# Low halves of columns and mixed rows move from VectorE to GpSimd, and the planner lets SBUF operations of the two engines run one at a time

## The chip, the cores and the metric

The kernel runs on one core of a Trainium2 chip. The core has a matrix engine (PE, with its weight loads as PEld), VectorE (DVE), ScalarE (ACT), GpSimd (POOL) and a queue engine (SP) that issues the DMAs. The metric is the device time of one execution in microseconds; lower is better. Times of instructions come from one profiled execution.

## What is computed

The reference is one decoder layer over 2048 tokens of width 1024, all in float32:

```
a = RMSNorm(x); u = a @ W_in -> conv value, conv gate, q, k, v (512 columns each)
conv = silu(LayerNorm(causal depthwise conv, width 31, of value * sigmoid(gate)))
attn = head-wise RMSNorm(stick-breaking attention of q, k, v; 8 heads of 64)
h = x + RMSNorm(concat(conv, attn) @ W_out)
out = h + RMSNorm((silu(f @ W_gate) * (f @ W_up)) @ W_down),  f = RMSNorm(h), inner width 2816
```

## The kernel before

**Number format.** PE multiplies float32 operands in a rounded form. To keep precision, an operand t is split into a high half H = round(t) and a low half L = t − H, and a product is made of three matmuls: H·H, H·L and L·H. ACT writes H with a copy (`AF.Copy`), and a subtraction writes L. Who subtracts depends on the place: VectorE where t lies in PSUM (`split`, lines 612 to 615), GpSimd for most weights (lines 580, 593, 1418, 1646), VectorE for the operands that the change touches.

**Tiling.** Tokens are worked in four groups of 512 (`g` = 0 to 3). For each group the input columns (8 blocks of 128 input features by 512 tokens, `xL` and `xH`) go through the input projection (`inproj`, matmuls at lines 622, 624, 626, 20 output tiles of 8 × 3 matmuls). Group 0 gets its columns by transposing scaled rows (`to_col`, line 630). Groups 1 to 3 read x already transposed from HBM: `turned` (lines 720 to 736) loads two blocks of columns at a time into `xcol` and multiplies them by the row factors `rb` on GpSimd (line 735); `prep` (lines 750 to 764) then lets ACT write H with the column factor gpm as its scale (line 761), and VectorE write L = xcol · gpm − H (line 762, a scalar_tensor_tensor with all operands in SBUF).

**Beside the projection** run two other streams. The convolution is done on VectorE: 30 taps per channel block of 128 and group, each a scalar_tensor_tensor into PSUM (`cv`, line 848). GpSimd copies the last 30 columns of a block's gated values to its front before the next group may write there (line 796); that copy has to wait for the last tap of the group before. The attention makes scores on PE (`z`, lines 931 and 932), a sigmoid on ACT (line 934), a scan along the keys on VectorE (`om`, lines 937 and 939), transposes on PE (`at`, line 957), the split of the transposed tile on ACT and VectorE (`TH` and `TL`, lines 614 and 615) and two matmuls into `o` (lines 962 and 963).

**Mixing.** When a group's convolution or attention is complete, `mixed` (lines 889 to 899) splits four blocks: H on ACT (line 895), L on VectorE (line 896). The output projection (`outproj`, matmuls at lines 1064 to 1066) reads them. There are eight such splits, two a group. The tiles `xH` and `xL` have two buffers each, which `prep`, `mixed`, `ffn_in` and `p4` share, so a low half is often written just when PE has read the old contents.

**Feed-forward part.** It starts within the mixing part (`c11`, `p4`) and takes the rest of the time, from about 1400 us on. It forms sums of operand blocks so that seven products do the work of eight. In its last part each step loads a piece of `w_down` and a hidden piece; ACT writes their high halves (lines 1645 and 1647), GpSimd one low half (line 1646) and VectorE the other (line 1648); VectorE adds up the rows that leave (line 1677).

**What sets the order.** All instructions are recorded in program order and then arranged. `Graph` gives each one a busy time (`cost`, line 193) and its dependencies; `forward` (line 317) plays the program engine by engine, taking the ready instruction of highest priority; `backward` makes new priorities; `arrange` repeats this 12 times, and `in_order` fixes the best order found for each engine. Each engine then runs its instructions strictly in that order, waiting for what is not ready. The numbers of `cost` and the rules of `forward` therefore change no instruction, only the order. In the version before, an instruction is called `wide` by `both_in_sbuf` (line 231) if it has two inputs of at least 128 elements and everything in SBUF; where wide instructions of VectorE and GpSimd overlap, lines 421 to 435 lengthen both by fractions of each other.

Of the kernel before, what the change touches and what calls it, by code (L numbers as in the profile page):

```python
# [10 lines left out]
F32 = mybir.dt.float32  # L11
F32R = mybir.dt.float32r
BF16 = mybir.dt.bfloat16
AF = mybir.ActivationFunctionType
ALU = mybir.AluOpType
# [139 lines left out]
def width(a):  # L155
    n = 1
    for _, c in a.ap[1:]:
        n *= int(c)
    return n
# [33 lines left out]
def cost(i, kind, eng, ins, outs):  # L193

    n = width(outs[0])
    if kind == "InstMatmult":
        if size_of(ins[0].dtype) == 4 and not str(ins[0].dtype).endswith("r"):
            return 109, 270
        b = max(width(ins[0]) * 0.443, 109)
        return b, b + 165  # L200
    src = [place(a) for a in ins]
    if eng == "Activation":
        b = n * 0.833 + (49 if src[0] == "PSUM" else 94) + (93 if len(ins) > 1 else 0)
        return b, b + 115
    if eng == "DVE":
        if kind == "InstTensorScalarPtr":
            if i.is_tensor_tensor_scan:
                b = 2.04 * n + 125
            elif i.is_scalar_tensor_tensor:
                b = 1.04 * n + 108  # L210
            else:
                b = 1.04 * n + 160 if place(outs[0]) == "PSUM" else 0.73 * n + 113
        elif kind == "InstBNStatsAggregate":
            b = 93
        elif kind in ("InstTensorReduce", "InstBNStats"):
            b = 1.04 * width(ins[0]) + 48
        elif kind == "InstTensorTensor":
            b = 1.04 * n + 60
        else:
            b = n + 100  # L220
        return b, b + 100
    if kind == "InstTensorTensor" and n >= 16:
        b = 2.35 * n + 35
    elif "pow" in str(getattr(i, "op", "")):
        b = 375 + 150 * n
    else:
        b = 125 if n < 16 else 215
    return b, b + 65


def both_in_sbuf(i, ins, outs):

    return sum(width(a) >= 128 for a in ins) > 1 and all(place(a) == "SB" for a in ins + outs)


class Op:
# [6 lines left out]
class Graph:  # L243


    def __init__(self, insts):
        self.ops, self.root, self.order, self.users = [], {}, {}, {}
        seen = {}
        for i in insts:
# [3 lines left out]
            if not outs:  # L253
# [1 line left out]
            eng, dma = str(i.engine).split(".")[-1], kind == "InstDMACopy"  # L255
            busy, late = (ISSUE, 0) if dma else cost(i, kind, eng, ins, outs)
            o = Op(len(self.ops), i, eng, dma, busy, late, width(outs[0]) * int(outs[0].ap[0][1]) * 4,
                   eng in ("DVE", "Pool") and not dma and both_in_sbuf(i, ins, outs))
            uses = [(a.bass_ap.tensor, box(a), place(a), w) for aps, w in ((ins, False), (outs, True)) for a in aps
                    if hasattr(a.bass_ap.tensor, "tag_meta")]  # L260
            for t, b, sp, w in uses:
# [55 lines left out]
    def forward(self, ops, prio, slots=True):  # L317
# [18 lines left out]
        busy = dict.fromkeys(ready, 0.0)  # L336
        start, stop = [None] * len(ops), [0.0] * len(ops)
        moved, flight = 0.0, []
        runs = {}
        ev = [(0.0, 0, 0, ())]  # L340
        for o in ops:
            if not need[o.n]:
# [28 lines left out]
        while ev:  # L371
# [24 lines left out]
            while look:  # L396
# [5 lines left out]
                while ready[e]:  # L402
# [12 lines left out]
                    if o.dma:  # L415
                        flight.append(n)
                        moved = max(t + AHEAD, moved) + o.size / RATE
                        stop[n] = moved + LAND
                    else:
                        more = 0.0  # L420
                        if o.wide if e == "DVE" else e == "Pool":
                            other = "Pool" if e == "DVE" else "DVE"
                            m, rest = runs.get(other), busy.get(other, 0.0) - t
                            if m is not None and rest > 0 and ops[m].wide:
                                if e == "DVE":
                                    more, push = min(1.2 * o.busy, 0.55 * rest), 0.28 * min(rest, 2 * o.busy)
                                elif o.wide:
                                    push = min(1.2 * rest, 0.55 * o.busy)
                                    more = 0.28 * (rest + push)
                                else:  # L430
                                    more, push = 0.8 * rest, 0.0
                                busy[e] += more
                                busy[other] += push
                                heapq.heappush(ev, (busy[other], 1, m, ()))
                        runs[e] = n
                        stop[n] = t + o.late + more
                    heapq.heappush(ev, (busy[e], 1, n, tuple(iss[n])))
                    for lag, then in fin[n].items():
# [65 lines left out]
def layer_kernel(ctx: ExitStack, tc: tile.TileContext, x, xT, g_pre_mix, w_in, conv_w, conv_b, ln_g, ln_b,  # L504
# [215 lines left out]
    def turned(T):  # L720
# [11 lines left out]
        r = row("xcol").rearrange("p (i t) -> p i t", i=2)  # L732
        nc.sync.dma_start(r, xT[g, kp])
        for i in range(2):
            nc.gpsimd.tensor_tensor(r[:, i, :], r[:, i, :], rbs[g], ALU.mult)
        rows["x", T] = r

# [12 lines left out]
    def prep(g):  # L750
# [7 lines left out]
        for k in range(KT):  # L758
            r = rows["x", g * TT + k // 2][:, k % 2, :]
            H = Hs[k // 4][:, k % 4, :]  # L760
            nc.scalar.activation(H, r, AF.Copy, scale=gpm[:, k:k + 1])
            nc.vector.scalar_tensor_tensor(Ls[k // 4][:, k % 4, :], r, gpm[:, k:k + 1], H.bitcast(F32), ALU.mult,
                                           ALU.subtract)
            yield 1

    def xtiles():
# [122 lines left out]
    def mixed(g, part, tiles=xtile):  # L889
# [3 lines left out]
        ms = [ma[g, p] if part else conv[g][:, p, :] for p in range(CB)]  # L893
        for k in range(CB):
            nc.scalar.activation(H[:, k, :], ms[k], AF.Copy)
            nc.vector.tensor_tensor(L[:, k, :], ms[k], H[:, k, :].bitcast(F32), ALU.subtract)
        if part:
            done.add(("mix", g))
        yield 1
# [912 lines left out]
```

## Time and profile before

| | us |
|---|---|
| median of 3 runs | 2397.09 |
| lowest and highest | 2396.34, 2401.08 |
| profiled execution, its own time | 2399.5 |
| span of its instructions | 2397.7 |
| PE busy | 2345.4 (98%) |
| DVE busy | 1762.9 (74%) |
| POOL busy | 1170.7 (49%) |
| ACT busy | 1167.3 (49%) |

The span runs from the first instruction's start to the last one's end; 1.8 us of the profiled execution lie around it. Busy times are means over stages with very different loads, so a stage has to be read by itself. Matmuls are pipelined and their ends are modelled: a PE that shows as busy can still issue a little more slowly than it could, and its idle time is a lower bound of what it lost. The granted TensorE clock was 0.996.

### The profile page before, as it was taken

How to read it: one execution, taken by the hardware profiler on the slowest of the kernel's cores; microseconds unless marked ns; L12 is line 12 of the kernel's file. 1: busy time of each engine (PE TensorE's matmuls, PEld its weight loads, DVE VectorE, ACT ScalarE, POOL GpSimd, SP SyncE). 2: the span in 40 equal slices, each digit the busy share in tenths (PEclk: the TensorE clock that was granted, in tenths of full speed). 3: DMA queues.
4: the chain of work that ended last, by engine and by line, in shares of the span. 5: the costliest groups of instructions: out<-in, count | busy, mean ns of one | idle time of the engine just before them, and what ended most of it. 6: DMA issues, size and time to landing. Idle time of an engine off the chain costs nothing.

```text
span 2397.7 us, 33860 instructions
## 1 busy us (share of the span) xinstructions
PE 2345.4 (98%) x11156; PEld 1930.4 (81%) x11156; DVE 1762.9 (74%) x2177; ACT 1167.3 (49%) x2078; POOL 1170.7 (49%) x994
## 2 busy tenths in 40 slices
PE   7999999999999999999999999999999999999998
PEld 5878878787888878788888887878888888888886
DVE  6897999899997699956741257888766664557556
ACT  4446555564665455455654554334332335454543
POOL 5462335432442334334610048678887445468656
PEclk9999999999999999999999999999999999999999
DMA  9888876897798899997889768899999667669665
GB/s 316 272 289 303 265 251 226 295 319 252 246 315 291 267 309 321 334 301 242 280 289 306 267 226 305 293 313 317 338 343 317 198 225 241 197 190 311 218 190 176
DMA packets 283791, 656.68 MB, mean 274 GB/s; under 512 B 34912, under 2 KB 35424, under 8 KB 283616
## 3 DMA queue, kind: packets, MB, share of 16 engines
q1 hardware_dynamic: 283616, 654.52, 81.4%
q8 instruction: 88, 1.44, 0.2%
q14 instruction: 87, 0.71, 0.1%
HBM read 460.40 MB, written 193.99 MB: 273 GB/s over the span
## 4 chain that ended last, share of the span: by engine, by line
PE 79%; DVE 13%; issue 3%; POOL 2%; DMA 2%; ACT 1%; SPq 0%; DVEq 0%; POOLq 0%; ACTq 0%
PE b L1128 17%; PE dps L1128 17%; PE c L1128 8%; PE inps L622 5%; PE inps L624 5%; PE inps L626 5%; DVE cv L848 4%; PE at L957 4%; PE p L1128 2%; PE o L963 2%; PE z L931 2%; PE ops L1065 2%; PE ops L1064 2%; PE z L932 2%; PE ops L1066 2%
## 5 line engine op out<-in xcount | busy, mean ns | idle before, releaser
L848 DVE SCALAR_TENSOR_TENSOR cv<-glu,cw,cv 128x512 f32<-128x512 f32 x464 | 347.6, 749 | 7.1
L1418 POOL TENSOR_TENSOR wL<-raw,wH 128x512 fp32r<-128x512 f32 x176 | 264.0, 1526 | 161.2 <-ACT wH L1417 161.2
L1648 DVE TENSOR_TENSOR xL__20078<-t__20080,xH__20077 128x512 fp32r<-128x512 f32 x154 | 196.5, 1279 | 146.8 <-ACT xH__20077 L1647 146.7
L1646 POOL TENSOR_TENSOR xL__20076<-t__20079,xH__20075 128x512 fp32r<-128x512 f32 x154 | 212.5, 1385 | 153.1 <-ACT xH__20075 L1645 151.3
L615 DVE TENSOR_TENSOR TL<-at,TH 128x512 fp32r<-128x512 f32 (+1 forms) x320 | 189.4, 601 | 124.2 <-ACT TH L614 114.5
L622 PE MATMUL inps<-xH,wL 128*128 128x512 f32 x640 | 258.5, 404 | 8.7 <-ACT sg L792 8.5
L626 PE MATMUL inps<-xL,wH 128*128 128x512 f32 x640 | 256.3, 401 | 0.0
L624 PE MATMUL inps<-xH,wH 128*128 128x512 f32 x640 | 255.9, 400 | 0.0
L939 DVE TENSOR_TENSOR_SCAN om<-z,om,one 128x512 f32<-128x512 f32 x168 | 213.2, 1276 | 49.4 <-ACT z L934 48.1
L1128 PE MATMUL dps<-xH__20075,xL__20078 128*128 128x512 f32 x616 | 240.1, 390 | 2.9 <-DVE xL__20078 L1648 2.9
L1128 PE MATMUL dps<-xH__20075,xH__20077 128*128 128x512 f32 x616 | 239.7, 389 | 0.0
L1128 PE MATMUL dps<-xL__20076,xH__20077 128*128 128x512 f32 x616 | 238.4, 389 | 0.0
L614 ACT ACTIVATE TH<-at 128x512 fp32r<-128x512 f32 (+1 forms) x320 | 168.5, 533 | 114.9 <-PE at L957 104.3
L934 ACT ACTIVATE z<-z 128x512 f32<-128x512 f32 (+2 forms) x320 | 167.0, 528 | 115.3 <-PE z L932 112.9
L576 ACT ACTIVATE wH<-raw 128x1024 fp32r<-128x1024 f32 x156 | 165.1, 1060 | 119.1 <-PE inps L626 59.7
L1645 ACT ACTIVATE xH__20075<-t__20079 128x512 fp32r<-128x512 f32 x154 | 97.1, 631 | 198.7 <-POOL xL__20076 L1646 135.8
L580 POOL TENSOR_TENSOR wL<-raw,wH 128x1024 fp32r<-128x1024 f32 x50 | 120.4, 2410 | 146.9 <-ACT wH L576 134.5
L957 PE MATMUL at<-idr,om 128*128 128x128 f32 x1088 | 185.2, 273 | 5.0 <-DVE om L939 2.5
L1417 ACT ACTIVATE wH<-raw 128x512 fp32r<-128x512 f32 x176 | 101.3, 623 | 146.1 <-PE b L1128 54.4
L957 PEld LDWEIGHTS at<-idr,om 128*128 128x128 f32 x1088 | 138.2, 141 | 41.3 <-DVE om L939 3.7
L1212 POOL TENSOR_TENSOR sum<-sum 128x512 f32<-128x512 f32 x88 | 117.1, 1330 | 98.5 <-DMA sum<-in_w_up_dram 48.8
L622 PEld LDWEIGHTS inps<-xH,wL 128*128 128x128 f32 x640 | 121.5, 190 | 32.8 <-issue 5.5
(294 smaller groups left out, 6018.5 us busy)
## 6 DMA issues: line engine op xcount, KB each, us to landing
wL<-wL SPq DMA_DIRECT2D x156, 512.0 KB, 5.4
raw<-in_w_in_dram SPq DMA_DIRECT2D x80, 512.0 KB, 5.7
t__20080<-u SPq DMA_DIRECT2D x154, 256.0 KB, 3.0
c<-c SPq DMA_DIRECT2D x88, 256.0 KB, 4.8
t__20079<-wd SPq DMA_DIRECT2D x88, 256.0 KB, 2.6
K<-kd SPq DMA_DIRECT2D x80, 256.0 KB, 4.6
V<-vd SPq DMA_DIRECT2D x80, 256.0 KB, 5.0
u<-accf SPq DMA_DIRECT2D x22, 768.0 KB, 6.6
```

The costliest lines, as they stand in the source:

```text
L614: nc.scalar.activation(H, ps, AF.Copy)
L615: nc.vector.tensor_tensor(L, ps, H.bitcast(F32), ALU.subtract)
L622: nc.tensor.matmul(ps, WL[:, kc], aH[t](k), start=k == 0, stop=False)
L624: nc.tensor.matmul(ps, WH[:, kc], aH[t](k), start=False, stop=False)
L626: nc.tensor.matmul(ps, WH[:, kc], aL[t](k), start=False, stop=k == KT - 1)
L848: nc.vector.scalar_tensor_tensor(to, gl[c][:, k:k + G], cw[:, c, k:k + 1], a, ALU.mult, ALU.add)
L939: nc.vector.tensor_tensor_scan(r, zr, one.to_broadcast([P, w]), hd_["prev"][j], ALU.mult, ALU.bypass)
L957: nc.tensor.transpose(pt[:, j * P:(j + 1) * P], u["A"][j][:, b * P:(b + 1) * P], id32)
L1128: return nc.tensor.matmul(ps, a, b, skip_group_check=True, **flags)
L1418: nc.gpsimd.tensor_tensor(l, t, f32(h), sub)
L1646: nc.gpsimd.tensor_tensor(WL, w, f32(WH), sub)
L1648: nc.vector.tensor_tensor(UL, t, f32(UH), sub)
```

## The change

Four edits are made.

1. In `turned`, ACT now multiplies each block of columns by its column factor gpm, in place, before GpSimd multiplies it by the row factors. That is one new ACT instruction for each of 24 blocks.
2. In `prep`, ACT writes H without a factor, and L = xcol − H is a plain subtraction on GpSimd instead of the scalar_tensor_tensor on VectorE: 24 instructions.
3. In `mixed`, L is subtracted on GpSimd instead of VectorE: 32 instructions.
4. In the planner, a VectorE instruction counts as wide if all its operands are in SBUF and its output has at least 128 elements, and every GpSimd instruction counts as wide. A wide instruction now begins, in the plan, only when the wide one before it, on either engine, has ended: `port` holds that time. The planned busy times of scans and of scalar_tensor_tensor grow by 15 and 17 ns.

```diff
@@ cost
-                b = 2.04 * n + 125
+                b = 2.04 * n + 140
             elif i.is_scalar_tensor_tensor:
-                b = 1.04 * n + 108
+                b = 1.04 * n + 125
@@
-def both_in_sbuf(i, ins, outs):
-    return sum(width(a) >= 128 for a in ins) > 1 and all(place(a) == "SB" for a in ins + outs)
+def in_sbuf(eng, ins, outs):
+    return eng == "Pool" or width(outs[0]) >= 128 and all(place(a) == "SB" for a in ins + outs)
@@ Graph.__init__
-                   eng in ("DVE", "Pool") and not dma and both_in_sbuf(i, ins, outs))
+                   eng in ("DVE", "Pool") and not dma and in_sbuf(eng, ins, outs))
@@ forward
-        runs = {}
+        port = 0.0
@@
-                        if o.wide if e == "DVE" else e == "Pool":
-                            other = "Pool" if e == "DVE" else "DVE"
-                            m, rest = runs.get(other), busy.get(other, 0.0) - t
-                            if m is not None and rest > 0 and ops[m].wide:
...
-                                busy[e] += more
-                                busy[other] += push
-                                heapq.heappush(ev, (busy[other], 1, m, ()))
-                        runs[e] = n
+                        if o.wide:
+                            more = max(port - t, 0.0)
+                            busy[e] += more
+                            port = busy[e]
@@ turned
         for i in range(2):
+            nc.scalar.activation(r[:, i, :], r[:, i, :], AF.Copy, scale=gpm[:, 2 * kp + i:2 * kp + i + 1])
             nc.gpsimd.tensor_tensor(r[:, i, :], r[:, i, :], rbs[g], ALU.mult)
@@ prep
-            nc.scalar.activation(H, r, AF.Copy, scale=gpm[:, k:k + 1])
-            nc.vector.scalar_tensor_tensor(Ls[k // 4][:, k % 4, :], r, gpm[:, k:k + 1], H.bitcast(F32), ALU.mult,
-                                           ALU.subtract)
+            nc.scalar.activation(H, r, AF.Copy)
+            nc.gpsimd.tensor_tensor(Ls[k // 4][:, k % 4, :], r, H.bitcast(F32), ALU.subtract)
@@ mixed
-            nc.vector.tensor_tensor(L[:, k, :], ms[k], H[:, k, :].bitcast(F32), ALU.subtract)
+            nc.gpsimd.tensor_tensor(L[:, k, :], ms[k], H[:, k, :].bitcast(F32), ALU.subtract)
```

Since the order is planned anew, instructions move on every engine. PE's order is close to the one before (its matmuls are the same 11,156 instructions); VectorE's and GpSimd's differ in many places. From line 421 on, the changed kernel's line numbers are smaller by 10 or 11: the taps of line 848 stand at 837, the low halves of lines 762 and 896 at 752 and 885, the copy of line 796 at 785.

The first place is VectorE at the split of group 0's convolution output. `xL<-acc` is the low half, `cv` a tap, `TL`, `qkL` and `vt` splits of PSUM tiles, `ot` a reduction after the attention of a head. Before:

```order
L979 TENSOR_REDUCE ot<-pf 128x4x64
L848 SCALAR_TENSOR_TENSOR cv<-glu_140,cw,cv 128x512
L615 TENSOR_TENSOR TL<-at,TH 128x128
L848 SCALAR_TENSOR_TENSOR cv<-glu_140,cw,cv 128x512
L896 TENSOR_TENSOR xL<-acc,xH 128x512
L848 SCALAR_TENSOR_TENSOR cv<-glu_140,cw,cv 128x512
L615 TENSOR_TENSOR qkL<-inps,qkH 128x512
L896 TENSOR_TENSOR xL<-acc,xH 128x512
```

Now, from the same reduction on:

```order
L968 TENSOR_REDUCE ot<-pf 128x4x64
L837 SCALAR_TENSOR_TENSOR cv<-glu_140,cw,cv 128x512 x2
L928 SCALAR_TENSOR_TENSOR om<-z,om,one 128x512
L604 TENSOR_TENSOR TL<-at,TH 128x128
L604 TENSOR_TENSOR vt<-vps,vt 128x4x64
L837 SCALAR_TENSOR_TENSOR cv<-glu_140,cw,cv 128x512
L604 TENSOR_TENSOR vt<-vps,vt 128x4x64
L837 SCALAR_TENSOR_TENSOR cv<-glu_140,cw,cv 128x512
L604 TENSOR_TENSOR TL<-at,TH 128x512 x2
```

The low halves are gone from between the taps and the attention's splits.

The second place is GpSimd at the columns of group 2. `xcol` is the multiplication by the row factors, `xL<-xcol` the low half that is new here, `wL` a weight's low half, `sum` a sum of feed-forward weights, `glu` the copy of 30 columns. Now:

```order
L725 TENSOR_TENSOR xcol<-xcol,rb 128x512 x7
L569 TENSOR_TENSOR wL<-raw,wH 128x1024
L752 TENSOR_TENSOR xL<-xcol,xH 128x512 x4
L725 TENSOR_TENSOR xcol<-xcol,rb 128x512
L1201 TENSOR_TENSOR sum<-sum 128x512
L546 TENSOR_SCALAR ms<-ss 128x1
L547 TENSOR_TENSOR rs<-ms,nhalf 128x1
L785 COPY glu_142<-glu_142 128x30
L752 TENSOR_TENSOR xL<-xcol,xH 128x512 x4
```

Before, no low half of columns stood in this queue. Now the second four stand behind a sum, which waits for its DMAs, and behind the copy, which waits for VectorE's last tap.

The third place is VectorE at the end of the program: `xL` is the low half of the hidden piece that PE's last products need, the scalar_tensor_tensor adds a finished row, `e__20083<-dps` (now `e__20107<-dps`) takes up PE's last results. Before:

```order
L1648 TENSOR_TENSOR xL__20078<-t__20080,xH__20077 128x512
L1677 SCALAR_TENSOR_TENSOR e__20086<-t__20082,rs,e__20086 128x512
L1648 TENSOR_TENSOR xL__20078<-t__20080,xH__20077 128x512
L1677 SCALAR_TENSOR_TENSOR e__20086<-e__20084,rs,e__20086 128x512
L1648 TENSOR_TENSOR xL__20078<-t__20080,xH__20077 128x512
L1677 SCALAR_TENSOR_TENSOR e__20086<-t__20082,rs,e__20086 128x512
L1648 TENSOR_TENSOR xL__20078<-t__20080,xH__20077 128x512
L1677 SCALAR_TENSOR_TENSOR e__20086<-e__20084,rs,e__20086 128x512
L1735 TENSOR_TENSOR e__20083<-dps,e__20083 128x512
```

Now:

```order
L1637 TENSOR_TENSOR xL__20102<-t__20104,xH__20101 128x512 x2
L1666 SCALAR_TENSOR_TENSOR e__20110<-t__20106,rs,e__20110 128x512
L1637 TENSOR_TENSOR xL__20102<-t__20104,xH__20101 128x512
L1724 TENSOR_TENSOR e__20107<-dps,e__20107 128x512
L1666 SCALAR_TENSOR_TENSOR e__20110<-e__20108,rs,e__20110 128x512
L1666 SCALAR_TENSOR_TENSOR e__20110<-t__20106,rs,e__20110 128x512
L1666 SCALAR_TENSOR_TENSOR e__20110<-e__20108,rs,e__20110 128x512
L1724 TENSOR_TENSOR e__20107<-dps,e__20107 128x512
```

Of the three additions to this pair of rows that stood ahead of the last low half, two now stand behind it.

More of the change, by code (lines that the diff above doesn't have):

```diff
@@ L420, in forward @@
                         more = 0.0
-                        if o.wide if e == "DVE" else e == "Pool":
-                            other = "Pool" if e == "DVE" else "DVE"
-                            m, rest = runs.get(other), busy.get(other, 0.0) - t
-                            if m is not None and rest > 0 and ops[m].wide:
[L425 to L431, printed above, removed]
-                                busy[e] += more
-                                busy[other] += push
-                                heapq.heappush(ev, (busy[other], 1, m, ()))
-                        runs[e] = n
+                        if o.wide:
+                            more = max(port - t, 0.0)
+                            busy[e] += more
+                            port = busy[e]
                         stop[n] = t + o.late + more
```

## Prediction

> **What bounds the kernel now.** I began with the page's busy times, then cut the span into stretches, since a share over 2400 us hides the stage that the change touches. The view of windows, with the busy us of each engine in each stretch:
>
> ```profile
> PE 2345.4 (98%) x11156; PEld 1930.4 (81%) x11156; DVE 1762.9 (74%) x2177; ACT 1167.3 (49%) x2078; POOL 1170.7 (49%) x994
> ...
> core 0: us, PE busy (x) PEld busy (x) DVE busy (x) ACT busy (x) POOL busy (x), PEclk, DMA share, GB/s
> 100.00:200.00 100.00, 98.21 (x501) 81.58 (x500) 95.66 (x148) 52.43 (x101) 50.59 (x49) 0.98 0.92 309
> 300.00:700.00 400.00, 391.23 (x1986) 320.99 (x1985) 390.40 (x538) 229.10 (x413) 156.33 (x169) 0.99 0.81 267
> 800.00:1000.00 200.00, 195.76 (x992) 159.54 (x991) 189.51 (x246) 103.51 (x182) 72.88 (x49) 1.00 0.90 305
> 200.00:300.00 100.00, 99.58 (x528) 82.84 (x527) 79.79 (x117) 55.54 (x103) 30.35 (x38) 1.00 0.85 271
> 700.00:800.00 100.00, 100.00 (x518) 83.55 (x517) 74.27 (x105) 54.00 (x98) 35.63 (x47) 1.00 0.90 309
> 1000.00:1400.00 400.00, 396.12 (x1938) 326.36 (x1937) 194.18 (x246) 225.08 (x387) 110.15 (x102) 1.00 0.85 286
> 1400.00:1600.00 200.00, 195.58 (x870) 159.71 (x869) 159.17 (x170) 80.97 (x137) 141.65 (x102) 1.00 0.80 276
> 1600.00:2300.00 700.00, 699.43 (x3081) 577.51 (x3080) 450.00 (x457) 282.34 (x510) 459.06 (x329) 1.00 0.78 263
> ```
>
> PE is the bound nearly everywhere; from 1600 to 2300 us it idles 0.57 us, and a faster helper can bring nothing there. Before 1400 us it shares the bound with VectorE. In the 700 us of the first three rows VectorE is 95 to 98% busy, and PE idles 1.79 + 8.77 + 4.24 = 14.8 us. In the 600 us of the next three VectorE has slack, and PE idles 0.42 + 0 + 3.88 = 4.3 us, or 0.72 per 100 us. PE's own waits between 300 and 700 us say on whom:
>
> ```profile
> PEld o L963 <- DVE TL L615: 5.3, 7, 2.6
> PE inps L622 <- ACT sg L792: 3.3, 2, 2.0
> PE o L963 <- DVE TL L615: 2.9, 3, 2.3
> PE at L957 <- DVE om L939: 1.6, 2, 1.2
> PEld inps L626 <- DVE xL L762: 0.5, 2, 0.2
> ```
>
> Mostly on VectorE's splits and scans of the attention. The low halves themselves (last row) hardly ever hold PE; they only stand in VectorE's queue ahead of what does.
>
> **What the change takes from VectorE.** The two groups between 300 and 700 us, and the spread of their durations over the whole run:
>
> ```profile
> L762 DVE SCALAR_TENSOR_TENSOR xL<-xcol,gpm,xH 128x512 fp32r<-128x512 f32 x16 | 15.3, 973 | 0.0
> L896 DVE TENSOR_TENSOR xL<-ma,xH 128x512 fp32r<-128x512 f32 x8 | 8.9, 1118 | 0.0
> L896 DVE TENSOR_TENSOR xL<-acc,xH 128x512 fp32r<-128x512 f32 x8 | 8.6, 1111 | 0.0
> ...
> L762 DVE SCALAR_TENSOR_TENSOR xL<-xcol,gpm,xH x24: 735/747/1784, 161.6 to 689.3; 128x512 fp32r<-128x512 f32 x24
> L896 DVE TENSOR_TENSOR xL<-acc,xH x16: 666/686/2559, 346.5 to 1368.4; 128x512 fp32r<-128x512 f32 x16
> L848 DVE SCALAR_TENSOR_TENSOR cv<-glu,cw,cv x464: 724/752/766, 31.7 to 1014.7; 128x512 f32<-128x512 f32 x155
> L735 POOL TENSOR_TENSOR xcol<-xcol,rb x24: 1273/1286/1737, 129.8 to 656.4; 128x512 f32<-128x512 f32 x24
> ```
>
> That is 15.3 + 8.9 + 8.6 = 32.8 us of VectorE's 390.4: its load falls to 357.6 of 400, or 89%, about what it is where PE hardly idles (80% between 200 and 300 us). The durations tell why the groups cost so much: alone one takes 0.69 to 0.75 us, but up to 2.56 us when it overlaps GpSimd. A tap, with one operand in PSUM, never does that (724 to 766 ns).
>
> How much of this reaches PE? If the three saturated rows fall to the idle rate of the others, 0.72 × 7 = 5.0 us stay of 14.8, a gain of **9.8 us**. The bounds are 0 (what holds the attention is latency, not VectorE's load) and 14.8 (nothing idles). Two short stretches support that the low halves are part of it: where those of groups 1 and 0 are made, PE lost 1.8 us in 17 and 2.4 us in 22.
>
> ```profile
> 157.00:174.00 17.00, 15.21 (x74) 12.39 (x73) 16.01 (x25) 11.14 (x20) 4.41 (x6) 0.90 0.91 296
> 344.00:366.00 22.00, 19.61 (x91) 16.02 (x90) 22.00 (x30) 12.25 (x22) 10.85 (x8) 0.92 0.84 242
> ```
>
> **What it adds to GpSimd.** By the row of line 735, a subtraction with both inputs in SBUF takes 1.29 us there: 56 of them are 72 us, 32 of them (41 us) between 300 and 700 us. GpSimd's load there grows from 156 to 198 us of 400, and between 100 and 200 us from 51 to 61. Its rate suffices for PE: the eight low halves of group 1 take 8 × 1.29 = 10.3 us on GpSimd, and PE spent 17 us on the stretch above. The last split, of group 3's attention output at 1384 to 1390 us, falls where GpSimd is empty. The new risk is its queue. A low half now waits behind instructions that wait for others, and PE's matmuls wait behind it; at the columns of group 2 it is the sum and the copy of 30 columns that stand ahead. GpSimd's waits before:
>
> ```profile
> POOL oT L1035 <- ACT oT L1027: 95.4, 22, 10.2
> POOL sum L1212 <- DMA sum<-in_w_up_dram: 48.8, 11, 9.6
> POOL glu L796 <- DVE cv L848: 27.7, 10, 6.3
> ```
>
> The copy waited 2.8 us on average and 6.3 at most. In a fixed order most of such a wait is time in which GpSimd had nothing to do, so I take 1.0 us in all, bounded by 0 and by 3 × 6.3 = 18.9 us (three groups' columns, each behind the longest wait).
>
> **What it adds to ACT.** The 24 new scalings cost 0.62 us each, by the plain copies from SBUF of line 895; the copies of line 761 shrink from 0.72 to 0.62:
>
> ```profile
> L895 ACT ACTIVATE xH<-acc x16: 615/620/632, 344.8 to 1365.7; 128x512 fp32r<-128x512 f32 x16
> L761 ACT ACTIVATE xH<-xcol,gpm x24: 705/716/735, 157.9 to 682.9; 128x512 fp32r<-128x512 f32 x24
> ```
>
> So 24 × 0.62 − 24 × 0.10 = 12.5 us more, on an engine that is 52 to 57% busy in these rows. Each scaling has to wait only for its DMA, since it comes before the row factors. I cost it at nothing; what hides it is ACT's 43% of idle time. If that cover went, it would show in PE's wait for the sigmoid `sg` (3.3 us above), by at most as much again. No DMA is added or moved past another by these edits themselves; SP's order is planned anew like the rest.
>
> **What the new order does elsewhere.** Between 1400 and 2300 us nothing but the order changes, and there PE idles 5.0 us in all: I take 0. At the end the trace has one stall that the order sets, in the timeline and in the waits of the last 58 us:
>
> ```profile
> 2374.63 1.78 DVE L1677 SCALAR_TENSOR_TENSOR e__20086<-e__20084,rs,e__20086 128x512 f32<-128x512 f32 x1
> 2375.82 3.40 POOL L1646 TENSOR_TENSOR xL__20076<-t__20079,xH__20075 128x512 fp32r<-128x512 f32 x2
> 2376.33 1.74 DVE L1648 TENSOR_TENSOR xL__20078<-t__20080,xH__20077 128x512 fp32r<-128x512 f32 x1
> 2377.99 1.77 DVE L1677 SCALAR_TENSOR_TENSOR e__20086<-t__20082,rs,e__20086 128x512 f32<-128x512 f32 x1
> 2378.13 0.50 PE L1128 MATMUL dps<-xH__20075,xL__20078 128*128 128x512 f32 x1 [2.03 <-DVE xL__20078 L1648]
> ...
> PE dps L1128 <- DVE xL__20078 L1648: 2.9, 2, 2.0
> ```
>
> The low halves that PE's last products need stand behind row additions which GpSimd's traffic stretches to 1.78 us (alone 0.75). In the new order two of these additions come after the last low half. PE's 2.9 us of waiting could go; but the additions then stand ahead of the results of PE's last products, and one of them stretched would cost 1.8 us. I take a gain of **1.5 us**, between −1.8 and 2.9.
>
> The sum: −9.8 − 1.5 + 1.0 = −10.3 us. The profiled execution took 2399.5 us, its span and 1.8 us around it, so 2389.2 us for such an execution. The median of the three runs is 2.4 us lower, 2397.09; from there I predict **2387 us**.
>
> **A rule that speaks against it.** The row of line 896 shows one subtraction taking 2.56 us instead of 0.69 while GpSimd works. The Trainium skill, Perfetto Trace Analysis, section Optimizing Scalar/DVE Operations, says that the two engines share a read port into SBUF, so that moving operations between them might not help. By it the time would be that of the first rival below; the row of line 848 shows how far it reaches here, since taps, VectorE's largest group, are not stretched at all.
>
> **Rivals.**
>
> (a) *The load goes and nothing follows* (chance 0.22). What PE waits for is the chain score, sigmoid, scan, transpose, split, whose length does not depend on VectorE's load, or what GpSimd's 72 us take back by stretching VectorE's other SBUF operations. For it: VectorE was idle before a scan for lack of a sigmoid now and then, and PE's idle time is only 2% even in the saturated rows. Against it: VectorE had no idle time of note there (9.6 us of 400). Time: 2397, give or take 4.
>
> (b) *Low halves late from GpSimd* (chance 0.19, the slower side). Each group's second four low halves stand behind the copy of 30 columns, hence behind VectorE's last tap. PE pays 18.9 us at the upper bound, and the balance is 2397.09 − 11.3 + 18.9 = 2404.7 us. It decides once the handovers cost more than 11.3 us together, 3.8 each. For it: two matmuls did wait for a low half of columns even before, so there is no lead to spend. Against it: the wait of the copy was GpSimd's own idle time, and the plan sees that dependency.
>
> (c) *All the idle goes* (chance 0.11). The 14.8 us, the 2.9 us at the end and the 4.3 us of the unsaturated rows: 22 us, or 2375. Some of what stays hidden in stretched matmuls might follow, so 2372 is its edge.
>
> **How the numbers follow.** The forecast has the rest, 0.48; its own range, with 5 us more or less of gain, is 2382 to 2393. About 0.2%, or 4.8 us, can be told from no change. Faster by more than that, below 2392.3: nine tenths of the forecast (0.43), all of (c) and a fifth of (a) (0.05), so 0.59. Slower, above 2401.9: 0.15 of (b) and 0.02 of (a), so 0.17. The rest, 0.24, is the same. The range has to reach (c) and (b): 2372 to 2404.
>
> **What would show it.** Right: VectorE at about 90% between 300 and 700 us, PE's idle time there near 3 us instead of 8.8, GpSimd near 200 us busy; waits of `o` for `TL` down by half; no wait of PE for a low half of columns or mixed rows above 1 us; no wait of PE at the end for the low half of line 1637 (1648 before). Wrong: PE idle as before with VectorE at 90% (then (a)), or PE waiting for GpSimd's low halves behind the copy (then (b)); or new gaps after 1400 us, which would be the order's doing and in no term of mine.

## The result and the profile after

The changed kernel took 2369.11 us (median of 4 runs, 2367.53 to 2371.6) against 2396.75 us (4 runs): a ratio of 0.9881, with a 95% interval of 0.9868 to 0.9893. That is 27.6 us, nearly three times the 10 us that were forecast, and outside the range of 2372 to 2404.

The first line of the page, for the changed kernel:

```profile
PE 2330.6 (99%) x11156; PEld 1927.4 (81%) x11156; DVE 1711.8 (72%) x2121; ACT 1179.5 (50%) x2102; POOL 1241.8 (52%) x1050
```

PE was *busy* for 2345.4 us before and for 2330.6 us now, with the same 11,156 matmuls. The spans differ by 2397.7 − 2365.4 = 32.3 us, so 14.8 us of the difference were no idle time at all. (The profiled execution of the kernel before, 2399.5 us, was one of its slower ones, and that of the changed kernel, 2367.53 us, its fastest; by medians the difference is 27.6 us. The stage times below are those of single executions and have some us of scatter.)

To see where the time went I use two landmarks that every version has: PE's last matmul on a split `TL` (the end of the attention) and its first `dps` (the last part of the feed-forward work). The view of one tile's instructions gives the first and last start of each; before:

```profile
L963 PE MATMUL o<-TL,V x320: 218/391/750, 76.2 to 1370.5; 128*128 128x512 f32 x128, 128*128 128x256 f32 x32
L1128 PE MATMUL dps<-xH__20075,xL__20078 x616: 389/389/504, 1966.1 to 2388.2; 128*128 128x512 f32 x154
```

And now:

```profile
L952 PE MATMUL o<-TL,V x320: 220/391/504, 73.1 to 1347.8; 128*128 128x512 f32 x128, 128*128 128x256 f32 x32
L1117 PE MATMUL dps<-xH__20099,xL__20102 x616: 387/389/504, 1935.8 to 2354.8; 128*128 128x512 f32 x154
```

So the mixer, up to the last `o`, fell from 1370.5 to 1347.8 us (−22.7); the stretch from there to the first `dps` from 595.6 to 588.0 (−7.6); the rest, to the end of the span, from 431.6 to 429.6 (−2.0). The view of windows up to the first landmark shows that both kernels had done the same work there (6698 and 6699 matmul records). Before:

```profile
0.00:1370.50 1370.50, 1334.70 (x6699) 1098.62 (x6700) 1080.94 (x1475) 745.01 (x1322) 503.70 (x509) 1.00 0.86 285
```

Now:

```profile
0.00:1347.80 1347.80, 1323.09 (x6698) 1094.75 (x6699) 1045.85 (x1423) 758.60 (x1346) 565.29 (x560) 1.00 0.86 290
```

Of the 22.7 us, PE's idle time gave 35.8 − 24.7 = 11.1, and its busy time 11.6. VectorE's load for the same work fell by 35.1 us. The stretches that the prediction used, now:

```profile
100.00:200.00 100.00, 96.76 (x509) 81.00 (x508) 96.28 (x143) 56.95 (x109) 59.12 (x57) 1.00 0.90 307
300.00:700.00 400.00, 397.51 (x2047) 329.18 (x2046) 385.29 (x530) 240.69 (x436) 197.26 (x210) 1.00 0.82 274
800.00:1000.00 200.00, 197.91 (x1000) 161.43 (x999) 191.86 (x257) 102.45 (x180) 75.69 (x47) 1.00 0.91 317
...
1400.00:1600.00 200.00, 199.91 (x898) 165.26 (x897) 166.53 (x182) 81.33 (x140) 154.65 (x109) 1.00 0.88 297
```

PE's idle time between 300 and 700 us fell from 8.8 to 2.5 us, yet VectorE is still 96% busy there: the faster order brings work forward into the stretch (2047 matmul records in it instead of 1986). Between 1400 and 1600 us, where nothing was moved, the idle time fell from 4.4 to 0.1 us. PE's waits from 100 to 1370 us, first before, then now:

```profile
PE o L963 <- DVE TL L615: 8.2, 9, 2.3
PE inps L622 <- ACT sg L792: 3.8, 3, 2.0
PE at L957 <- DVE om L939: 2.5, 4, 1.2
```

```profile
PE po L984 <- DVE ot L976: 3.7, 2, 2.8
PE inps L611 <- ACT sg L781: 2.4, 3, 1.1
...
PE o L952 <- DVE TL L604: 0.5, 1, 0.5
PE at L946 <- DVE om L928: 0.4, 1, 0.4
```

The waits for splits are nearly gone, those of the transposes (`at`) for scans fell from 2.5 to 0.4 us, and no wait for a low half from GpSimd has come in their place. The wait for `ot`, a VectorE operation behind the attention, grew from 0.5 to 3.7 us.

**What a stall cost beside its idle time.** Three of the long waits before were followed by a stretch at half the granted clock. Windows of the kernel before around them (the column behind the engines is the granted clock):

```profile
165.00:169.00 4.00, 3.86 (x17) 3.22 (x16) 3.37 (x7) 2.15 (x5) 0.00 (x0) 0.61 0.93 274
353.00:357.00 4.00, 3.91 (x15) 3.18 (x14) 4.00 (x5) 2.10 (x4) 2.67 (x2) 0.57 1.00 337
459.00:463.00 4.00, 4.00 (x13) 3.19 (x14) 1.54 (x4) 1.54 (x2) 0.19 (x1) 0.57 1.05 346
```

The lost clock is 4 × (0.39 + 0.43 + 0.43) = 5.0 us, nearly all of it in "busy" time. The changed kernel has no such stretch between 61 and 2360 us: its mean clock of 0.998 over 2365.4 us is a loss of about 4.7 us, and 5 × 0.34 + 8 × 0.44 = 5.2 us of loss lie in two stretches outside, the second behind the last matmul:

```profile
56.00:61.00 5.00, 3.74 (x11) 2.99 (x12) 0.73 (x2) 0.87 (x2) 1.77 (x1) 0.66 0.96 277
2360.00:2368.00 8.00, 0.00 (x0) 0.00 (x0) 1.41 (x2) 0.00 (x0) 0.40 (x1) 0.56 0.32 131
```

The lost clock explains 5.0 of the 11.6 us; the rest of the busy time was not taken apart.

### The profile page after: what moved, and what is told of

It is laid out like the page before. It is cut to its first block, busy times and chain, and to the rows that moved or that the text cites. A ratio compares the mean times of both kernels' runs of the same rounds, so it can differ in the third digit from the quotient of the medians.

```text
span 2365.4 us, 33884 instructions
## 1 busy us (share of the span) xinstructions
PE 2330.6 (99%) x11156; PEld 1927.4 (81%) x11156; DVE 1711.8 (72%) x2121; ACT 1179.5 (50%) x2102; POOL 1241.8 (52%) x1050
## 4 chain that ended last, share of the span: by engine, by line
PE 91%; DVE 4%; DMA 2%; POOL 1%; issue 1%; ACT 1%; SPq 1%; POOLq 0%; DVEq 0%; ACTq 0%
PE b L1117 22%; PE dps L1117 17%; PE c L1117 10%; PE inps L611 5%; PE inps L613 5%; PE inps L615 5%; PE at L946 4%; PE p L1117 3%; PE ops L1053 2%; PE ops L1054 2%; PE ops L1055 2%; PE z L921 2%; PE z L920 2%; PE o L951 2%; PE o L952 2%
```

## The experiments

The question was how much of the gain belongs to the moved operations (edits 1 to 3), how much to the planner (edit 4), and how either reaches PE. All ratios are to the kernel before, with 95% intervals, from runs of both on the same chip. Letters name theories; each is told in the expectation that was written before the run.

### Each half of the change alone

*Planner alone*: the diff's hunks in `cost`, `Graph` and `forward`, none in `turned`, `prep`, `mixed`.

> The new planner (edit 4) with every operation where it was before. Theory M (the moved operations bring what is gained up to 1350 us of PE's work, some 22.7 us of the 32.3 us by which the profiled executions differ; the new plan brings the 9.6 us after that point): 2397 - 9.6 = 2387 us, with VectorE still above 95% busy between 300 and 700 us, and the stall for wL and accf between 1400 and 1600 us gone. Theory P (the plan brings it all): 2369 us. Theory L (any new order moves the time by some us either way, and the gain after 1350 us is such a draw): anything from 2385 to 2405 us.

Measured: 2395.35 us, ratio 0.9997 (0.9989 to 1.0006). No gain. The last `o` came at 1376.1 us, later than before; from there to the first `dps` 588.0 us, the rest 429.5 us, both as short as with the whole change. One stall stands out in the mixer. Timelines of VectorE, GpSimd and PE in this run:

```profile
396.01 10.69 DVE L885 TENSOR_TENSOR xL<-ma,xH 128x512 fp32r<-128x512 f32 x1
406.62 0.68 DVE L604 TENSOR_TENSOR TL<-at,TH 128x512 fp32r<-128x512 f32 x1
```

```profile
395.04 9.88 POOL L724 TENSOR_TENSOR xcol<-xcol,rb 128x512 f32<-128x512 f32 x8
404.89 1.25 POOL L1201 TENSOR_TENSOR sum<-sum 128x512 f32<-128x512 f32 x1
```

```profile
407.35 0.80 PE L952 MATMUL o<-TL,V 128*128 128x512 f32 x1 [9.09 <-DVE TL L604]
```

And the windows around it:

```profile
395.00:407.00 12.00, 3.26 (x19) 2.43 (x17) 12.00 (x5) 2.30 (x4) 11.14 (x10) 0.83 0.40 156
403.00:413.00 10.00, 5.65 (x15) 4.59 (x16) 7.47 (x7) 1.82 (x3) 3.14 (x3) 0.50 0.07 26
407.00:413.00 6.00, 5.65 (x15) 4.59 (x16) 3.47 (x6) 1.82 (x3) 0.00 (x0) 0.50 0.11 43
```

A low half of mixed rows that takes 0.69 us alone stood for 10.69 us, until eight multiplications of GpSimd (1.24 us each, not slowed) and the sum behind them, which ended at 406.1 us, were through. The split behind it kept PE waiting for 9.1 us. The granted clock was at a half from 403 to 413 us; PE waited until 407.35 us, so what the clock cost beside the wait is about 6 × 0.5 = 3.0 us.

*Moves alone*: the hunks in `turned`, `prep`, `mixed`, with the old planner.

> The moved operations (edits 1 to 3) with the planner of before. Theory M: 2397 - 22.7 = 2374 us, with a stall between 1400 and 1600 us and at the end as before. Theory P: 2397 us or more, since the low halves go to GpSimd without a plan that keeps the two engines apart. Theory L: 2369 to 2390 us, with the losses anywhere.

Measured: 2384.09 us, ratio 0.995 (0.9938 to 0.9963); last `o` at 1351.6 us, then 596.6 us and 434.1 us. The mixer gained 18.9 us, and what lies behind it is as slow as before, as theory M had it. The whole time is 10 us above what theory M gave: the mixer gained 3.8 us less, what lies behind it took 3.5 us more, and the theory had taken stage times of a profiled execution of 2399.5 us off a median of 2397 us.

*Columns alone and mixed rows alone*, each with the new planner:

> New planner, low halves of columns on GpSimd with the factor on an ACT pass (edits 1, 2 and 4); low halves of mixed rows stay on VectorE. The two groups that the change moves out of the 300 to 700 us stretch cost VectorE 15.3 us (columns) and 17.5 us (mixed rows). Theory M, with gain shared out by that load: plan only less 0.47 of 22.7 us = 10.6 us, so about 2376 us. Theory P: 2369 us as with all edits.

> New planner, low halves of mixed rows on GpSimd (edits 3 and 4); columns as before, with no new ACT pass. Theory M by load: plan only less 0.53 of 22.7 us = 12 us, so about 2375 us. Theory P: 2369 us.

Measured: 2367.75 us (0.9883, 0.9869 to 0.9896) and 2375.76 us (0.9916, 0.9902 to 0.9929). The columns alone do as much as all three moves, as theory P had it; the mixed rows alone came out where theory M had them. In these plans the gain is not shared out by VectorE's load, and the parts do not add: planner 1 us, moves 13 us, both 28 us. Each is a single plan, and plans scatter, as shown further down.

### The same order, with other engines

Every edit also makes the planner find another order. To hold the order still I let the planner see an instruction as if it stood on its other engine, and put it where the planner had it:

```diff
@@ Graph.__init__
             eng, dma = str(i.engine).split(".")[-1], kind == "InstDMACopy"
+            if i.name in PLANNED:
+                eng, kind, like = PLANNED[i.name]
@@ in_order
-        if o.eng in prev:
+        eng = str(o.ins.engine).split(".")[-1]
+        if eng in prev:
```

The order of all other instructions is then the same on every engine.

*Low halves back on VectorE, in the new order:*

```diff
-            nc.gpsimd.tensor_tensor(Ls[k // 4][:, k % 4, :], r, H.bitcast(F32), ALU.subtract)
+            nc.vector.tensor_tensor(Ls[k // 4][:, k % 4, :], r, H.bitcast(F32), ALU.subtract)
+            planned(nc, "Pool", "InstTensorTensor")
```

(and the same in `mixed`).

> The changed kernel with the order that was planned for it kept on every engine, and only the 56 low halves (24 of columns, 32 of mixed rows) put back on VectorE, as subtractions, each between the instructions that run there at the time planned for it on GpSimd. ACT's factor pass stays. Theory N (the new order is good because of the moved operations): VectorE gets 56 x 0.69 = 39 us more, of which PE loses what the run with the moves alone gained over before until 1350 us of work, 19 us, and lock-outs behind trains of GpSimd's can add to it: 2369 + 19 = 2388 us or more, with single low halves above 2 us. Theory O (the order itself, not the engine, carries the gain): 2369 to 2373 us.

Measured: 2396.49 us, ratio 0.9992 (0.9983 to 1.0001): all of the gain gone, 28.0 us later at the last `o` (1375.8 us). PE waited 9.2 us for `TL` again:

```profile
PE o L966 <- DVE TL L616: 9.2, 9, 1.9
PE po L998 <- DVE ot L990: 2.8, 1, 2.8
PE ops L1067 <- DVE big L1072: 2.5, 1, 2.5
```

The order alone does not carry the gain: theory O fell.

*The same places with one input:* `nc.vector.tensor_scalar(L, H, 1.0, None, ALU.mult)` instead of the subtraction.

> As the run with the low halves back on VectorE in the new order, but each of the 56 reads one operand from SBUF only: it multiplies the high half by 1 instead of subtracting. The subtraction of the high half is left out, so the low half is not one. VectorE keeps an instruction in each of the 56 places, but none with two SBUF inputs. Theory L (lock-out: a VectorE instruction with two inputs from SBUF stands still while GpSimd works, and that is what the 56 cost): back to 2369 to 2373 us, and no instruction of the 56 above 0.8 us. Theory V (VectorE's load costs): between the run with the subtractions and 2369 us by load, since 56 x about 0.5 us stay: 2369 + 0.5/0.69 x 19 = about 2383 us.

Measured: 2383.49 us, ratio 0.9939 (0.9927 to 0.9952), where theory V had it. The close hit is part luck: theory V shared out 19 us for the 56 subtractions, and these had just cost 2396.49 − 2369.11 = 27.4 us; by that scale it would have said about 2389. The subtraction is left out here. These instructions have one input and single ones are still held up beside GpSimd, so theory L fell:

```profile
L764 DVE TENSOR_SCALAR xL<-xH x24: 398/419/2356, 158.5 to 686.9; 128x512 fp32r<-128x512 f32 x24
```

*Low halves on GpSimd, in the old order:*

```diff
-            nc.vector.scalar_tensor_tensor(Ls[k // 4][:, k % 4, :], r, gpm[:, k:k + 1], H.bitcast(F32), ALU.mult,
-                                           ALU.subtract)
+            nc.gpsimd.tensor_tensor(Ls[k // 4][:, k % 4, :], r, H.bitcast(F32), ALU.subtract)
+            planned(nc, "DVE", "STT")
```

> The kernel before with its order kept on every engine, and only the 56 low halves moved to GpSimd, each at the time planned for it on VectorE; no ACT pass. The low half of a column is xcol - H without the column factor: that factor is left out there. Theory N: most of what the moves alone gained up to 1350 us, without any new order: 2397 - 19 = 2378 us, and the stalls from 1400 to 1600 us and at the end as before. Theory O: 2397 us or slower, since GpSimd's queue was not planned for them.

The column factor is left out of the low halves of columns here. Measured: 2402.52 us, ratio 1.0022 (1.0013 to 1.0031), slower than before. VectorE was relieved, 363.32 us busy between 300 and 700 us instead of 390.4, and PE gained nothing by it. Its waits from 100 to 1370 us:

```profile
PE vps L824 <- POOL step L818: 5.9, 3, 2.4
PE inps L636 <- ACT sg L806: 4.0, 4, 2.1
PE o L978 <- DVE TL L629: 3.9, 6, 1.8
...
PE inps L640 <- POOL xL L776: 1.4, 2, 0.8
```

The waits for `TL` halve, and waits for GpSimd's `step` (differences of v) and for its low halves, none of them of note before, take their place: 7.3 us.

*One split moved, in the order of the planner alone:* only the four low halves of group 0's attention output go to GpSimd.

> The run with the new planner alone, its order kept, with only the four low halves of group 0's attention output moved to GpSimd. There one low half on VectorE (line 885) took 10.69 us beside eight multiplications of GpSimd (9.88 us), PE waited 9.5 us for a split behind it, and the granted clock then fell to a half for 10.24 us. Theory L (lock-out, then clock): the one stall cost 9.5 + 5.1 = 14.6 us, so 2395 - 14.6 = 2381 us, no half clock near 400 us. If the stall has another cause: 2395 us as before, and a stall in the same place.

Measured: 2387.78 us, ratio 0.9957 (0.9944 to 0.9971). The stall is gone, and so is the half clock:

```profile
395.00:407.00 12.00, 11.19 (x58) 9.01 (x57) 9.10 (x15) 5.11 (x9) 12.00 (x10) 1.00 0.38 142
407.00:413.00 6.00, 5.57 (x25) 4.12 (x23) 5.62 (x5) 2.37 (x3) 5.92 (x5) 1.00 0.53 143
```

The place and the cause were right; the price was 7.6 us and not 14.6. The expectation counted the whole stretch at half clock on top of the wait, though PE was still waiting in its first part: 9.1 + 3.0 = 12.1 us is what the stall cost. Other losses then follow: 1.4 us for `big` and 0.8 us for one of the moved low halves between 400 and 430 us, and a longer stretch at half clock (0.66 from 574 to 584 us; the run with the planner alone had 0.83 at the same work, from 585 to 595 us).

### Which part of the planner

Rule alone and planned times alone, with and without the moves: two lines of `cost`, or the hunks of `Graph` and `forward`.

> All moved operations, and of the planner's edits only the rule that wide instructions of the two engines begin one after the other; planned times of scans and of scalar_tensor_tensor as before. With the moves under the planner of before 2384 us and with everything 2369 us. Theory R (the rule brings the part of the plan): 2369 us, no stall between 1400 and 1600 us. Theory T (the planned times bring it): 2384 us, with it.

> All moved operations, and of the planner's edits only the longer planned times of scans and scalar_tensor_tensor; the old rule for overlaps. Theory R: 2384 us, with the stall between 1400 and 1600 us. Theory T: 2369 us without it.

> No operation moved, only the longer planned times. Another order for the operations of before, so a draw of what an order does by itself: theory M (moved operations carry what comes before 1350 us) says 2390 to 2402 us; theory S (orders scatter as much as the change gains) says that it may lie anywhere from 2369 to 2402 us.

> No operation moved, only the new rule for overlaps. Theory M with the rule carrying the part after 1350 us: 2385 to 2392 us, unless a low half on VectorE is caught behind a train of GpSimd's as in the run with the whole new planner alone (then 2395). Theory S: anywhere from 2369 to 2402 us.

With the runs above these make a complete table: time (median), last `o`, from there to the first `dps`, from there to the end of the span, in us. The three stages are those of the profiled execution; for the planned times with nothing moved that was the fastest of 11 (2389.79 us). The rows come from several chips, on which the kernel before had medians of 2396.7 to 2398.05 us.

| planner | nothing moved | all moved |
|---|---|---|
| old | 2396.75: 1370.5, 595.6, 431.6 | 2384.09: 1351.6, 596.6, 434.1 |
| planned times | 2394.28: 1361.2, 593.8, 433.0 | 2380.93: 1353.1, 593.7, 433.6 |
| rule | 2383.28: 1365.2, 588.0, 429.6 | 2379.6: 1359.8, 587.5, 429.8 |
| both | 2395.35: 1376.1, 588.0, 429.5 | 2369.11: 1347.8, 588.0, 429.6 |

The ratios of the four new ones are 0.9925 (0.9911 to 0.9939) for rule and moves, 0.993 (0.9918 to 0.9943) for times and moves, 0.9985 (0.9977 to 0.9994) for the times alone and 0.9941 (0.9929 to 0.9954) for the rule alone. The times alone lie within both theories' ranges (M and S), so that run did not tell them apart; the rule alone came out 1.7 us below theory M's range. Two things can be read off. Behind the mixer the rule decides: 588.0, 588.0, 587.5, 588.0 us with it and 593.7 to 596.6 without, and 429.5 to 429.8 against 431.6 to 434.1 to the end. The planned times change nothing there beside the rule; without it they take 2 to 3 us off the middle stage. The waits of PE's weight loads (PEld) between 1400 and 1600 us in the run with moves and old rule, but new times, show what the rule takes away:

```profile
PEld b L1128 <- POOL wL L1418: 3.2, 2, 1.9
PEld b L1128 <- DVE accf L1425: 2.3, 4, 0.8
PEld b L1128 <- DVE glu L1425: 1.0, 1, 1.0
```

How it does so can be seen in the busy time of the feed-forward part's operations on VectorE that a helper records under one line (1425, with the rule 1414), from the last `o` to the first `dps`: the same 411 instructions in every run. The number behind the length of each window is their busy time. The kernel before, the moves alone, the rule alone, and the changed kernel:

```profile
1370.50:1966.10 595.60, 375.56 (x411) 1.00 0.83 286
1351.60:1948.20 596.60, 371.93 (x411) 1.00 0.83 286
1365.20:1953.20 588.00, 356.52 (x411) 1.00 0.85 290
1347.80:1935.80 588.00, 359.57 (x411) 1.00 0.85 290
```

In the two orders planned by the rule they take 12 to 19 us less: the same operations on VectorE are held up less in this stage, on the chip and not only in the plan.

In the mixer the four orders of either set lie 12 to 15 us apart (1361.2 to 1376.1; 1347.8 to 1359.8), and their means 1368.3 − 1353.1 = 15.2 us. So the moves are worth some 15 us there in the mean of four pairs, but the pairs range from 5.4 to 28.3 us, and four do not fix the mean well. What holds throughout is the sign: each of the four orders with the moves is shorter than each without. The 22.7 us of the change (old planner and nothing moved against both edits and all moved) include what two single orders happened to be worth. Theory R held for what lies behind the mixer; for the whole time neither R nor T did, since the orders of the mixer scatter.

### Does PE follow VectorE's load?

The two runs with low halves put back were 28.0 and 16.0 us later at the last `o`, with VectorE 32.4 and 20.6 us busier up to there (the changed kernel's 1045.85 us against 1078.22 and 1066.40):

```profile
0.00:1375.80 1375.80, 1334.46 (x6698) 1097.16 (x6699) 1078.22 (x1474) 759.44 (x1346) 505.11 (x509) 0.99 0.85 284
```

```profile
0.00:1363.80 1363.80, 1329.85 (x6698) 1094.25 (x6699) 1066.40 (x1474) 758.83 (x1346) 501.83 (x509) 1.00 0.85 286
```

That is 0.8 to 0.9 us of time for each us of VectorE's. Four more runs asked whether taking load off brings something like it.

*First taps on ACT, in the changed kernel's order* (and, for the second, planned anew):

```diff
-            nc.vector.tensor_scalar(a, gl[c][:, 0:G], cw[:, c, 0:1], cb_[:, c:c + 1], ALU.mult, ALU.add)
+            nc.scalar.activation(a, gl[c][:, 0:G], AF.Identity, scale=cw[:, c, 0:1], bias=cb_[:, c:c + 1])
```

> The changed kernel in its own order, with only the first tap of each channel block and group (16 instructions, 0.81 us each on VectorE) computed by ACT instead, at the place planned for it. Theory V (PE's pace in the mixer follows VectorE's busy time, 0.5 to 0.6 us for each us): 16 x 0.81 = 12.9 us off, so 2369 - 6.5 to 7.7 = 2361 to 2363 us. Theory D (what the runs with low halves put back cost was the disturbed order): 2367 to 2372 us.

> The same with the order planned anew. Theory V: about 2362 us, and since orders of the same operations differed by 5 us either way, 2357 to 2367 us. Theory D: 2364 to 2374 us.

> Low halves of columns on GpSimd with the factor pass, low halves of mixed rows on VectorE, the whole new planner, and the first taps on ACT. Theory V: the run without the first taps moved took 2368 us; less 7 us, with 5 us of scatter either way: 2356 to 2366 us. Theory D: 2363 to 2373 us.

Measured: 2369.29 us (0.9881, 0.9868 to 0.9895), 2371.37 us (0.989, 0.9877 to 0.9904) and, with the columns alone, 2374.63 us (0.9901, 0.9886 to 0.9917). In the fixed order VectorE's load up to the last `o` fell from 1045.85 to 1036.44 us, and the time did not move. By itself that decides little, since the changed kernel has few waits left that a freer VectorE could shorten; the kernel before has them all.

*Short one-input low halves in the old order:*

> The kernel before in its own order, with each of the 56 low halves on VectorE reading one operand (the high half times 1; the subtraction is left out, so the low half is not one). They took 51.7 us before and 28.5 us in this form in the new order: 23 us off VectorE, nothing on GpSimd. Theory V: 2397 - 12 to 14 = 2383 to 2385 us. Theory D, or if an order made for the longer instructions cannot use the time: 2393 to 2397 us, as moving them to GpSimd in this order did not gain.

Measured: 2397.28 us, ratio 0.9997 (0.9988 to 1.0006). VectorE's load fell by 12.1 us up to the last `o`:

```profile
0.00:1367.50 1367.50, 1332.77 (x6698) 1098.37 (x6699) 1068.86 (x1475) 745.00 (x1322) 499.74 (x509) 1.00 0.86 285
```

and the last `o` came 3.0 us earlier, which the whole time does not show. In all four runs theory V missed; theory D had the first two and was exceeded by 1.6 us with the columns alone and by 0.3 us here. Adding work to an order that was planned without it delays PE; taking work out of an order that was planned with it brought next to nothing in these runs. So the moves act through the plan: with them the planner finds orders of the mixer that are shorter, some 15 us in the mean. That it is VectorE's load that does this is not shown: the two orders planned anew with the first taps off VectorE as well, hence with still less load, have their last `o` at 1354.0 and 1355.6 us, later than the same kernels without that step (1347.8 and 1347.6 us). Their VectorE load up to there is 7 us lower, and the difference is within the scatter of plans. It may as well be that the operations that can be held up beside GpSimd are gone from between the attention's steps; no run tells the two apart under a new plan.

## Why the prediction was wrong

- **What bounds the kernel** was right where it named PE's waits for splits and scans behind VectorE between 100 and 1000 us. What it took from that was wrong: it read PE's lost time as its idle time (14.8 us, "nothing idles") and made that the upper bound. This is the first step that failed. Up to the last `o` only 11.1 of the 22.7 us were idle time. The other 11.6 us were busy time, 5.0 us of it clock lost behind stalls. The sign of it stood in the prediction's own rows: the two short stretches it quotes have a granted clock of 0.90 and 0.92, so 17 × 0.10 + 22 × 0.08 = 3.5 us were lost there beside the 4.2 us of idle time that it counted. Its "mostly on VectorE's splits and scans" rests in part on a row of weight loads (5.3 us) that wait for the same splits: of PE's own waits there, 4.5 us were for splits and scans and 3.3 us for ACT's `sg`.
- **"Between 1400 and 2300 us nothing but the order changes: I take 0"** is the second step that failed: 7.6 us between the last `o` and the first `dps`, where it had 5.0 us of idle time in view. The table of planners shows that the new rule brings this, whatever is moved. The prediction costed the planner's edit at the end of the program alone.
- **How the load reaches PE** was a mechanism put too simply: the load falls and PE's idle rate falls to that of other stretches. The runs in a fixed order show that a lower load by itself brought nothing (ratio 0.9997, and 1.0022 where GpSimd's queue added waits, in the old order), and that the order by itself brought nothing either (0.9992 with the low halves back on VectorE). Where the sum has 9.8 us the profiled executions show 22.7 us, moves and new plan together; over four plans the moves bring 15.2 us there in the mean, between 5.4 and 28.3.
- **VectorE at 90% between 300 and 700 us** was wrong: 96%. Work has moved forward into the stretch, for example 201 of VectorE's taps instead of 190. PE's idle time "near 3 us" (2.5), GpSimd "near 200 us" (197) and no wait for low halves from GpSimd above 1 us were right; the waits for `TL`, forecast to fall by half, fell from 8.2 to 0.5 us. That PE's idle time fell as forecast while VectorE stayed at 96% says that VectorE's share of busy time was no measure of what PE waits for.
- **The end**: 1.5 us forecast, 2.0 found from the first `dps` on. The rule does it: the orders without it take 431.6 to 434.1 us there whether or not anything is moved, those with it 429.5 to 429.8.
- **Low halves late from GpSimd** (1.0 us, rival b): no wait in the changed kernel. The mechanism is real all the same: in the old order, with GpSimd's queue not planned for them, waits for GpSimd came to 7.3 us, and the moves brought a loss. In orders planned with the moves no such wait came, nor in the one by the old planner (2384.09 us).
- **ACT**: the scaling takes 0.713 us and not 0.62 (a copy with a factor, as line 761 had shown), so 17.1 − 2.1 = 15.0 us instead of 12.5. Hidden, as costed: the waits for `sg` fell from 3.8 to 2.4 us.

```profile
L724 ACT ACTIVATE xcol<-xcol,gpm x24: 710/713/782, 41.1 to 510.0; 128x512 f32<-128x512 f32 x24
L751 ACT ACTIVATE xH<-xcol x24: 612/627/637, 155.5 to 667.8; 128x512 fp32r<-128x512 f32 x24
```

- **Rival (a)**, that the load goes and nothing follows, is what happens in the old order. **Rival (c)**, that all idle time goes (2375), was nearest to the time and still too small, for the same reason as the forecast. The rule of the Trainium skill (Perfetto Trace Analysis, section Optimizing Scalar/DVE Operations) that such a move might not help is a caution that did not come true with a new plan: with each of the four planners the moves brought something, 12.7, 13.4, 3.7 and 26.2 us by the table's medians. In the old order it did (ratio 1.0022).

## What to carry to other kernels

On a matrix engine that shows as 98% busy, idle time is a lower bound of what the stalls cost: count matmul records to a landmark that both versions share, and look at the granted clock behind each stall. Where a planner sets the order, the price of an operation cannot be had from its duration alone: here freed time was not used without a new plan, and a new plan scatters by itself (12 to 15 us, over four plans of the same instructions): judge a move by several plans, and an order by holding it fixed. A planner's rule can also be worth something in stages that it was not changed for, so cost its effect on every stage that has idle time left.

## What the hardware showed

- A VectorE subtraction with both inputs in SBUF was held up for 10.69 us, through nine GpSimd operations in a row (eight multiplications of 1.24 us each and a sum of 1.25 us) that were not slowed themselves. The Trainium skill, SBUF — State Buffer, section Who interferes with whom, says that the pair of ports shared by the two engines is an exclusive lock. This trace agrees, and shows that the wait can last for a whole train of instructions.
- Waits of PE of about 2 us were followed by some 3 us at half the granted clock in three places of the kernel before (0.57 to 0.61 over 4 us), and one of 9.1 us went with 10 us of it, from within the wait on (0.50 from 403 to 413 us). A wait of 2.8 us, the changed kernel's for `ot`, was not followed by any (clock 1.00 from 100 to 200 us). What decides is not shown.
- "One at a time" is a rule of the plan only, and the chip keeps to it in part. Between the mixer and the first `dps` the same 411 VectorE operations got shorter by it (375.56 to 356.52 us with the rule alone). In the last part the low halves still overlap with GpSimd as before; before, and now:

```profile
L1648 DVE TENSOR_TENSOR xL__20078<-t__20080,xH__20077 128x512 fp32r<-128x512 f32 x154 | 196.5, 1279 | 146.8 <-ACT xH__20077 L1647 146.7
```

```profile
L1637 DVE TENSOR_TENSOR xL__20102<-t__20104,xH__20101 128x512 fp32r<-128x512 f32 x154 | 200.0, 1300 | 160.5 <-ACT xH__20101 L1636 156.0
```

A subtraction that takes 0.69 us alone still takes 1.30 us on average there.
